# Forming the low part of every fourth weight chunk with an accumulating transfer

## The chip, the cores and the metric

The kernel runs on one core of a Trainium2 chip. The metric is the device time of one execution in microseconds. Three runs of the kernel before the change took 1153.44, 1153.44 and 1154.11 us.

## What is computed

The kernel computes two layers of a streaming encoder on 256 rows of 1024 values, all in float32. Each layer is a feed-forward block, a mixer (a state-space scan, chunk attention and gates, all fed by one input projection) and a second feed-forward block. Each of the three has a norm before it and a norm after it.

```python
for l in range(DEPTH):                       # DEPTH = 2
    f1 = swiglu(rmsnorm(x, g[0]), w_gate, w_up, w_down)
    x = x + 0.5 * rmsnorm(f1, g[1])
    m = hybrid_mixer(rmsnorm(x, g[2]), w_in, ..., w_o)
    x = x + rmsnorm(m, g[3])
    f2 = swiglu(rmsnorm(x, g[4]), w_gate, w_up, w_down)
    x = x + 0.5 * rmsnorm(f2, g[5])
```

## The kernel before

All large products run on TensorE in the format fp32r. To keep float32 accuracy, each float32 matrix is split in two: a high part, which is the matrix rounded to fp32r, and a low part, which is the matrix minus its high part. A product then takes three matmuls: high by high, high by low, low by high.

The weights come from memory in 368 chunks of 128 x 1024 float32 values (512 KB each). `weight(i)` (line 443) makes one chunk ready: SyncE loads it into a buffer `raw` (line 452), ScalarE rounds it into `wh` (line 454, through `act`, line 358), and VectorE writes `wl = raw - wh` (line 455, through `tt`, line 365). There are 4 buffers `raw`, 8 buffers `wh` and 8 buffers `wl`. The loads are issued in the order of the chunks, on SyncE's queue.

The 256 rows are two tiles of 128, t = 0 and t = 1. Each chunk is used once by each tile, with six matmuls of 512 columns each time; the first one that reads `wl` is the second of the six. Tile 1 works on a chunk three chunks after tile 0 (`LAG = 3`), so that one tile's matmuls run while the other tile's norm, transposes or activations are under way.

Nothing of the order is written by hand. The code first records all operations in a graph; `schedule` (line 197) then simulates five queues (TensorE, ScalarE, VectorE, GpSimd and the loads) with a cost for each operation, a latency for each pair of engines and a due time that is counted back from the matmuls. Of the operations that can start, the one with the earliest due time goes first. The order in which this plan starts the operations becomes each engine's program order. Chunk conversions are due a margin of 7.558 us (`MARGIN["conv"]`) before the matmul that needs them. GpSimd's part is small: it sets buffers, and in each norm it raises one value per row to the power -1/2 (`pow`, line 376), between VectorE's sum and VectorE's scaling.

Of the kernel before, what the change touches and what calls it, by code (L numbers as in the profile page):

```python
# [12 lines left out]
F32 = mybir.dt.float32  # L13
# [3 lines left out]
AF = mybir.ActivationFunctionType  # L17
ALU = mybir.AluOpType
# [31 lines left out]
HOP = 0.2  # L50
DMA_LAT = 2.1
DMA_RATE = 350e3


class Buf:
# [6 lines left out]
class View:  # L62
# [50 lines left out]
    def ap(self):  # L113
        t = self.buf.tile
        for s in self.steps:
            t = s(t)
        return t
# [11 lines left out]
class Graph:  # L129
# [62 lines left out]
    def latency(self, a, b):  # L192
        if a.eng == "dma":
            return DMA_LAT if b.eng != "dma" else 0.0
        return LAT.get((a.eng, b.eng), HOP)

    def schedule(self):
        for o in reversed(self.ops):
            d = 1e9
            for s in o.succ:  # L200
                m = MARGIN.get(o.stream, 0.0) if s.stream != o.stream else 0.0
                d = min(d, s.due - m - o.cost - self.latency(o, s))
            o.due = d if o.due is None else max(o.due - CAP, min(o.due, d))
            o.wait = len(o.deps)
            o.est = 0.0
        queue = {c: [] for c in ORDERED}
        for o in sorted(self.ops, key=lambda o: (o.due, o.n)):
            for b in o.bufs:
                if b.cls in queue and b.order is None:
                    queue[b.cls].append(b)  # L210
                    b.order = len(queue[b.cls])
        self.taken = {c: [False] * (len(q) + 1) for c, q in queue.items()}
        self.low = {c: 1 for c in queue}
        free = {e: 0.5 for e in ("pe", "act", "dve", "pool", "dma")}
        slots = {c: [0.0] * n for c, n in SLOTS.items()}
        cand = {e: [] for e in free}
        for o in self.ops:
            if not o.wait:
                cand[o.eng].append(o)
        table, order, left = None, [], len(self.ops)  # L220
        while left:
            best = None
            for e, lst in cand.items():
                t = None
                for o in lst:
                    s = max(free[e], self.fits(o, slots))
                    if t is None or s < t:
                        t = s
                if t is not None and t < 1e9 and (best is None or t < best[0]):
                    best = (t, e)  # L230
            if best is None:
                raise RuntimeError(f"no operation can start, {left} left")
            t, e = best
            pick = None
            for o in cand[e]:
                s = max(t, self.fits(o, slots))
                if s <= t + (LOOK if o.cost < 0.9 else 0.0):
                    key = (o.due + (s - t), o.n)
                    if pick is None or key < pick[0]:
                        pick = (key, o, s)  # L240
            _, o, s = pick
            cand[e].remove(o)
            cost = o.cost
            if o.func is not None and table not in o.func:
                cost += 1.28
                table = o.func[0]
            if e == "pe" and s < COLD:
                cost *= 2
            o.start, o.end = s, s + cost
            free[e] = o.end  # L250
            for b in o.bufs:
                if b.slot is not None:
                    continue
                if b.cls in slots:
                    fs = slots[b.cls]
                    i = min(range(len(fs)), key=lambda q: fs[q])
                    b.slot = i
                    fs[i] = 1e9
                    if b.cls in self.taken:
                        tk = self.taken[b.cls]  # L260
                        tk[b.order] = True
                        while self.low[b.cls] < len(tk) and tk[self.low[b.cls]]:
                            self.low[b.cls] += 1
                else:
                    b.slot = 0
                    if b.cls not in slots:
                        slots[b.cls] = [1e9]
            for b in o.bufs:
                b.left -= 1
                b.end = max(b.end, o.end + (DMA_LAT if e == "dma" else HOP))  # L270
                if not b.left:
                    slots[b.cls][b.slot] = b.end
            for q in o.succ:
                q.wait -= 1
                q.est = max(q.est, o.end + self.latency(o, q))
                if not q.wait:
                    cand[q.eng].append(q)
            order.append(o)
            left -= 1
        self.total = max(o.end for o in order)  # L280
        order.sort(key=lambda o: o.start)
        return order
# [29 lines left out]
class Kern:  # L312
# [24 lines left out]
    def dma(self, out, in_, after=()):  # L337
        n = math.prod(out.shape if not isinstance(out, View) else (out.parts[1] - out.parts[0], *out.idx.shape))
        isv = isinstance(out, View)
        return self.g.op("dma", 4 * n / DMA_RATE, [out] if isv else [], [] if isv else [in_],  # L340
                         lambda: self.nc.sync.dma_start(out=ap(out), in_=ap(in_)), after=after)  # L341

    def memset(self, eng, out, v, after=()):
        name = "gpsimd" if eng == "pool" else "vector"
        self.g.op(eng, 0.1 + out.free_size() / (1100 if eng == "pool" else 1080), [out], [],
                  lambda: getattr(self.nc, name).memset(out.ap(), v), after=after)
# [96 lines left out]
    def weight(self, i):  # L443
        if i not in self.ws:
            g = self.g
            keep = (g.stream, g.rank, g.due)
            self.mode("conv" if i >= 6 else "conv0", "main")
            raw = g.buf("raw", [P, 1024])
            wh, wl = g.buf("wh", [P, 1024], F32R), g.buf("wl", [P, 1024], F32R)
            parts = [slice(0, 512), slice(512, 1024)] if i < 2 else [slice(0, 1024)]  # L450
            for s in parts:
                self.last_raw = self.dma(raw[:, s], self.w_d[i][:, s], after=[self.last_raw] if self.last_raw else [])
            for s in parts:
                self.act(wh[:, s], raw[:, s], AF.Copy)
                self.tt(wl[:, s], raw[:, s], wh[:, s].bitcast(F32), ALU.subtract)
            self.ws[i] = (wh, wl)
            g.stream, g.rank, g.due = keep
        return self.ws[i]
# [685 lines left out]
```

## Time and profile before

| | us |
|---|---|
| median of 3 runs | 1153.44 |
| lowest and highest run | 1153.44, 1154.11 |
| span of the profiled execution, first to last instruction | 1151.6 |
| median of the runs less that span | 1.8 |

The span is that of one execution taken by the profiler; the runs' times hold, besides, what lies before the first and after the last instruction. In the profile, PE is TensorE's matmuls and PEld its weight loads, DVE is VectorE, ACT is ScalarE, POOL is GpSimd and SP is SyncE, which only issues transfers here. L365 is line 365 of the kernel. Lines such as L358 and L365 are helpers, so that a group of instructions is told by the names of what it writes and reads: `wl<-raw,wh` reads `raw` and `wh` and writes `wl`.

### The profile page before, as it was taken

The page shows a single profiled execution, that of the slowest core. Times are in us where ns is not written, and L with a number is a line of the kernel's source. Part 1 is how long each engine was busy: PE and PEld are TensorE (multiplying, and loading weights), DVE is VectorE, ACT ScalarE, POOL GpSimd, SP SyncE. Part 2 cuts the span into 40 slices and gives each one's busy share as a digit, 9 for nine tenths or more (in the row PEclk, how much of TensorE's full clock was granted, in tenths as well). Part 3 has the DMA queues.
Part 4 walks back from the last instruction along what each step waited for, and adds up shares of the span by engine and source line. Part 5 has one row for each costly group of instructions (what it writes and reads, how often), then busy time and mean ns, then how long its engine had stood idle before and what let it go on. Part 6 is the DMA issues. An engine that isn't in the chain of part 4 may idle for free.

```text
span 1151.6 us, 15538 instructions
## 1 busy us (share of the span) xinstructions
PE 1140.8 (99%) x5872; PEld 914.0 (79%) x5872; DVE 788.6 (68%) x1190; ACT 606.3 (53%) x894; POOL 19.8 (2%) x53
## 2 busy tenths in 40 slices
PE   8999999999999999999999999999999999999997
PEld 7887888877788888888888878887777888888886
DVE  6995557896958854655799734578779678544553
ACT  6565445648555554444555643455685446444442
POOL 1000000000000000000000000000000000000000
PEclk9999999999999999999999999999999999999999
DMA  8754565553255665555565546654534565555551
GB/s 291 252 195 159 183 219 166 181 164 130 86 189 178 207 200 184 186 182 184 187 220 193 184 150 200 204 177 147 166 110 145 184 198 163 192 192 181 190 165 37
DMA packets 60267, 205.02 MB, mean 178 GB/s; under 512 B 7072, under 2 KB 7840, under 8 KB 60192
## 3 DMA queue, kind: packets, MB, share of 16 engines
q1 hardware_dynamic: 60192, 204.03, 53.7%
q8 instruction: 46, 0.75, 0.3%
q14 instruction: 29, 0.24, 0.1%
HBM read 202.96 MB, written 1.05 MB: 177 GB/s over the span
## 4 chain that ended last, share of the span: by engine, by line
PE 94%; ACT 4%; issue 1%; DMA 0%; SPq 0%; DVE 0%; POOLq 0%; POOL 0%; DVEq 0%
PE ps L400 89%; PE ps L414 4%; ACT utz L358 2%; PE ps L406 1%; ACT blk L358 1%; ACT wh L358 1%; DMA x<-in_x_dram 0%; SPq L341 0%; DVE x L380 0%; POOLq L1139 0%; POOL s L376 0%; DVEq L1139 0%; DVE s L388 0%; POOLq L376 0%
## 5 line engine op out<-in xcount | busy, mean ns | idle before, releaser
L400 PE MATMUL ps<-wh,blk 128*128 128x512 f32 x2944 | 916.4, 400 | 0.0
L400 PEld LDWEIGHTS ps<-wh,blk 128*128 128x128 f32 x2944 | 548.0, 188 | 122.6 <-issue 0.3
L365 DVE TENSOR_TENSOR wl<-raw,wh 128x1024 fp32r<-128x1024 f32 (+1 forms) x370 | 448.7, 1217 | 281.9 <-ACT wh L358 280.6
L358 ACT ACTIVATE wh<-raw 128x1024 fp32r<-128x1024 f32 (+1 forms) x370 | 389.7, 1055 | 374.5 <-PE ps L400 334.1
L400 PE MATMUL ps<-wl,blk 128*128 128x512 f32 x1472 | 551.7, 399 | 0.0
L400 PEld LDWEIGHTS ps<-wl,blk 128*128 128x128 f32 x1472 | 274.8, 188 | 61.1 <-issue 0.3
L358 ACT ACTIVATE blk<-ps 128x512 fp32r<-128x512 f32 (+3 forms) x136 | 78.1, 583 | 121.5 <-PE ps L414 103.3
L365 DVE TENSOR_TENSOR blk<-ps,blk 128x512 fp32r<-128x512 f32 (+2 forms) x104 | 69.0, 666 | 36.1 <-ACT blk L358 34.9
L414 PE MATMUL ps<-ident,blk 128*128 128x128 f32 x432 | 76.8, 273 | 0.2
L414 PEld LDWEIGHTS ps<-ident,blk 128*128 128x128 f32 x432 | 57.0, 140 | 20.1 <-ACT blk L358 1.0
L358 ACT ACTIVATE blk<-ps,s 128x512 f32<-128x512 f32 (+1 forms) x80 | 52.5, 658 | 27.6 <-PE ps L400 25.6
L380 DVE SCALAR_TENSOR_TENSOR blk<-ps,s,blk 128x512 f32<-128x512 f32 (+1 forms) x48 | 33.8, 703 | 15.3 <-PE ps L400 11.5
L376 POOL TENSOR_TENSOR s<-s,mhalf 128x1 f32<-128x1 f32 x24 | 13.8, 574 | 804.0 <-DVE s L388 799.1
L358 ACT ACTIVATE blk<-blk,s 128x128 f32<-128x128 f32 (+1 forms) x64 | 25.8, 444 | 0.0
L400 PEld LDWEIGHTS ps<-utz,bt 128*128 128x128 f32 x128 | 18.1, 191 | 4.0 <-ACT utz L358 2.8
L365 DVE TENSOR_TENSOR blk<-blk,blk 128x512 f32<-128x512 f32 (+3 forms) x38 | 21.1, 577 | 0.1
L358 ACT ACTIVATE utz<-blk 32x128 f32<-32x128 f32 x64 | 20.1, 314 | 1.0
L358 ACT ACTIVATE blk<-blk 64x128 f32<-64x128 f32 (+2 forms) x44 | 17.1, 393 | 6.5 <-DVE blk L380 6.0
L365 DVE TENSOR_TENSOR blk<-blk,e 128x512 f32<-128x512 f32 x32 | 20.3, 677 | 0.0
L400 PE MATMUL ps<-utz,bt 128*128 128x128 f32 x128 | 19.2, 278 | 1.0 <-ACT utz L358 0.8
L365 DVE TENSOR_TENSOR blk<-ps,e 128x512 f32<-128x512 f32 x32 | 19.9, 677 | 0.0
L856 DVE TENSOR_TENSOR_SCAN blk<-mt,blk 128x512 f32<-128x512 f32 x16 | 18.6, 1203 | 0.0
(106 smaller groups left out, 349.2 us busy)
## 6 DMA issues: line engine op xcount, KB each, us to landing
raw<-in_wall_dram SPq DMA_DIRECT2D x366, 512.0 KB, 3.5
gain<-in_gains_dram SPq DMA_DIRECT2D x22, 256.0 KB, 4.6
blk<-in_bias_dram SPq DMA_DIRECT2D x8, 256.0 KB, 5.0
raw<-in_wall_dram SPq DMA_DIRECT2D x4, 256.0 KB, 3.5
blk<-in_sp_dram SPq DMA_DIRECT2D x4, 256.0 KB, 4.0
x<-in_x_dram SPq DMA_DIRECT2D x3, 256.0 KB, 5.5
out_dram<-x SPq DMA_DIRECT2D x2, 256.0 KB, 2.0
out_dram<-x SPq DMA_DIRECT2D x2, 192.0 KB, 2.1
```

Of the source, the lines that this page charges most:

```text
L358: self.nc.scalar.activation(out=out.ap(), in_=in_.ap(), func=func, **k)
L365: lambda: self.nc.vector.tensor_tensor(out=out.ap(), in0=a.ap(), in1=b.ap(), op=op))
L376: lambda: self.nc.gpsimd.tensor_tensor(out=out.ap(), in0=a.ap(), in1=b.ap(), op=ALU.pow))
L380: return self.g.op("dve", cost, [out], [a, s, b], lambda: self.nc.vector.scalar_tensor_tensor(out=out.ap(), in0=a.ap(), scalar=ap(s), in1= ...
L400: return self.g.op("pe", cost, [out], [lhsT, rhs], lambda: self.nc.tensor.matmul(out.ap(), lhsT=lhsT.ap(), rhs=rhs.ap(), start=start, stop ...
L406: self.nc.tensor.matmul(out.ap(), lhsT=lhsT.ap(), rhs=rhs.ap(), start=start, stop=stop)
L414: lambda o=o, s=s: self.nc.tensor.transpose(o.ap(), s.ap(), self.ident.ap()))
L856: self.g.op("dve", 0.6, [o], [mt, z], lambda o=o, z=z: self.nc.vector.tensor_tensor_scan(out=o.ap(), data0=mt.ap(), data1=z.ap(), initial= ...
```

## The change

From chunk 16 on, every fourth chunk (i = 16, 20, ..., 364: 88 of the 368) gets its low part in another way. ScalarE still rounds `raw` into `wh`. ScalarE then writes `-wh` into `wl`, and GpSimd issues a transfer from `raw` to `wl` that adds what it carries to what stands there, so that `wl` becomes `raw - wh`. VectorE's subtraction is left out for these chunks. The planner is told of the new operation: it costs GpSimd 1.2 us, and what waits for it (TensorE's matmuls on `wl`, the next load into `raw`) may go 6.0 us after that.

```diff
+ADD_LAT = 6.0
...
     def latency(self, a, b):
         if a.eng == "dma":
             return DMA_LAT if b.eng != "dma" else 0.0
+        if a.func == "dma":
+            return ADD_LAT
         return LAT.get((a.eng, b.eng), HOP)
...
-            if o.func is not None and table not in o.func:
+            if e == "act" and o.func is not None and table not in o.func:
...
-                b.end = max(b.end, o.end + (DMA_LAT if e == "dma" else HOP))
+                b.end = max(b.end, o.end + (DMA_LAT if e == "dma" else ADD_LAT if o.func == "dma" else HOP))
...
+    def dma_add(self, out, in_):
+        return self.g.op("pool", 1.2, [out], [out, in_],
+                         lambda: self.nc.gpsimd.dma_start(out=out.ap(), in_=in_.ap(), accum_op=ALU.add), func="dma")
...
+            if i >= 16 and i % 4 == 0:
+                self.act(wh, raw, AF.Copy)
+                self.act(wl, wh.bitcast(F32), AF.Copy, scale=-1.0)
+                self.dma_add(wl.bitcast(F32), raw)
+                parts = []
             for s in parts:
                 self.act(wh[:, s], raw[:, s], AF.Copy)
                 self.tt(wl[:, s], raw[:, s], wh[:, s].bitcast(F32), ALU.subtract)
```

## Rows read from the trace of the kernel before

**Rows 1.** The page: span, then each engine's busy time, share, instructions.

```profile
span 1151.6 us, 15538 instructions
PE 1140.8 (99%) x5872; PEld 914.0 (79%) x5872; DVE 788.6 (68%) x1190; ACT 606.3 (53%) x894; POOL 19.8 (2%) x53
```

**Rows 2.** The page: the chain that ended last, by engine.

```profile
PE 94%; ACT 4%; issue 1%; DMA 0%; SPq 0%; DVE 0%; POOLq 0%; POOL 0%; DVEq 0%
```

**Rows 3.** Waits of PEld and PE: total us, times, longest us.

```profile
PEld ps L400 <- issue: 10.2, 38, 0.4
PEld ps L414 <- DMA x<-in_x_dram: 3.1, 3, 2.0
PEld ps L400 <- ACT utz L358: 2.8, 6, 0.7
PEld ps L414 <- ACT blk L358: 1.0, 2, 0.5
PEld ps L406 <- DVE blk L365: 0.7, 2, 0.4
PEld ps L406 <- DVE wl L365: 0.4, 1, 0.4
PEld ps L400 <- DVE wl L365: 0.2, 1, 0.2
PE ps L400 <- ACT utz L358: 0.8, 2, 0.4
```

**Rows 4.** Groups by line and shape: count | busy us, mean ns | idle before.

```profile
L365 DVE TENSOR_TENSOR wl<-raw,wh 128x1024 fp32r<-128x1024 f32 x366 | 446.0, 1223 | 278.9 <-ACT wh L358 277.7 <-issue 0.3
L358 ACT ACTIVATE wh<-raw 128x1024 fp32r<-128x1024 f32 x366 | 387.2, 1059 | 371.6 <-PE ps L400 334.1 <-issue 15.8 <-DMA raw<-in_wall_dram 14.6
L376 POOL TENSOR_TENSOR s<-s,mhalf 128x1 f32<-128x1 f32 x24 | 13.8, 574 | 804.0 <-DVE s L388 799.1 <-DVE blk L365 4.9
```

**Rows 5.** Timeline of ACT: start us, us, what, idle before and its releaser.

```profile
320.60 1.06 ACT L358 ACTIVATE wh<-raw 128x1024 fp32r<-128x1024 f32 x1 [0.64 <-PE ps L400]
321.56 0.67 ACT L358 ACTIVATE blk<-ps,s 128x512 f32<-128x512 f32 x1
...
440.12 1.06 ACT L358 ACTIVATE wh<-raw 128x1024 fp32r<-128x1024 f32 x1 [1.72 <-PE ps L400]
442.90 1.06 ACT L358 ACTIVATE wh<-raw 128x1024 fp32r<-128x1024 f32 x1 [1.72 <-PE ps L400]
445.68 1.06 ACT L358 ACTIVATE wh<-raw 128x1024 fp32r<-128x1024 f32 x1 [1.72 <-PE ps L400]
```

**Rows 6.** Timelines of PE and DVE in the same stretch.

```profile
442.93 0.39 PE L400 MATMUL ps<-wl,blk 128*128 128x512 f32 x1
443.16 0.39 PE L400 MATMUL ps<-wh,blk 128*128 128x512 f32 x1
443.39 0.40 PE L400 MATMUL ps<-wl,blk 128*128 128x512 f32 x1
...
441.21 1.23 DVE L365 TENSOR_TENSOR wl<-raw,wh 128x1024 fp32r<-128x1024 f32 x1 [1.56 <-ACT wh L358]
```

**Rows 7.** Issues by kind: KB each, median us to landing; queue; landings of `raw`.

```profile
raw<-in_wall_dram SPq DMA_DIRECT2D x366, 512.0 KB, 3.5
gcol<-in_g_dram SPq DMA_DIRECT2D x1, 4.0 KB, 1.6
...
q1 hardware_dynamic: 60192, 204.03, 53.7%
...
L341 SPq DMA_DIRECT2D raw<-in_wall_dram x370: 327/328/921, 1.6 to 1117.7; - x185
...
DMA to landing us min/median/max: 2.6/3.5/8.0
```

**Rows 8.** Waits of SP's queue and of ACT's conversions.

```profile
SPq L341 <- DVE wl L365: 820.4, 313, 15.9
...
ACT wh L358 <- PE ps L400: 334.1, 237, 3.0
```

**Rows 9.** Windows: busy us (and count) of each engine, PEclk, DMA share, GB/s.

```profile
core 0: us, PE busy (x) PEld busy (x) DVE busy (x) ACT busy (x) POOL busy (x), PEclk, DMA share, GB/s
225.00:296.00 71.00, 70.92 (x494) 54.90 (x494) 57.37 (x98) 48.34 (x105) 0.55 (x1) 1.00 0.38 127
410.00:560.00 150.00, 150.00 (x669) 121.23 (x668) 85.40 (x115) 67.39 (x73) 0.00 (x0) 1.00 0.56 188
793.00:864.00 71.00, 70.92 (x493) 55.04 (x492) 57.27 (x97) 48.34 (x105) 0.55 (x1) 1.00 0.39 127
```

**Rows 10.** The same windows for `wl` alone: subtractions stand under DVE.

```profile
225.00:296.00 71.00, 28.76 (x70) 13.16 (x70) 19.39 (x17) 1.00 0.38 127
...
793.00:864.00 71.00, 28.34 (x69) 12.98 (x69) 19.27 (x16) 1.00 0.39 127
```

## The prediction

> **What bounds the kernel now.** I read the page's busy shares first: PE is busy 99% of a span of 1151.6 us, DVE 68%, ACT 53% and POOL 2% [rows 1]. A busy share alone proves little, so the chain that ended last comes next: 94% of it is PE, 4% ACT, and DVE rounds to 0% [rows 2]. Then the waits of the matmul engine, which say what PE could win at all [rows 3]: after the inputs' arrival (3.1 us) it waited for ACT 2.8 + 1.0 + 0.8 us and for DVE 0.7 + 0.4 + 0.2 us in the rows shown, some 6 us in all, and the longest single wait was 0.7 us. The 10.2 us under "issue" are PE's own. PE runs at its upper clock level, 2.4 GHz (granted share 1.00 in the windows, [rows 9]), and in a dense stretch one 512-column matmul follows the other every 0.23 us [rows 6]. So the reader is to see a kernel that ends when PE has gone through its list, with hardly a gap in it.
>
> The conversions run ahead of PE and are held back by it: 237 of ACT's roundings into `wh` waited for PE, 334.1 us in all [rows 8], that is for a `wh` buffer that PE had not yet let go. In a dense stretch one chunk is rounded every 2.78 us (440.12, 442.90, 445.68; [rows 5]), which is PE's pace of 12 matmuls per chunk at 0.23 us [rows 6].
>
> **What the change removes.** 88 subtractions of 1223 ns each [rows 4]: 107.6 us of DVE. DVE is hardly on the chain [rows 2], and PE's waits for it come to 1.3 us [rows 3]. I put the gain at 0; its upper bound is 1.3 us directly, and about 6 us if a less loaded DVE also shortened every wait for ACT.
>
> **What it adds on ACT.** 88 copies `-wh` of the shape of the rounding, 1059 ns each [rows 4], though the next instruction starts 0.96 us after one (320.60 to 321.56, [rows 5]): 84 to 93 us, which brings ACT from 53% to about 61%. In dense stretches this is covered by ACT's idle time: in 410 to 560 us it is busy 67.4 of 150 us [rows 9] and would be so about 80, with 13 more copies. Cover is thin in one stretch of each layer, 225 to 296 and 793 to 864 us, where ACT is busy 48.3 of 71 us and DVE 57.4 [rows 9]. There 17 and 16 subtractions stand [rows 10], so 4 copies land in each stretch, 8 in all, 8 x 1.06 = 8.5 us if each were in PE's way, 0 if none is. For the value between I let the 93 us fall on the chain as ACT's work there does now, 4% [rows 2]: 3.7 us; and I take half of it, 1.8 us, because the planner sees ACT's cost and sets other matmuls before a late one. This half is a choice, not a row.
>
> **What it adds on GpSimd's queue and the transfer engines.** No row shows a transfer issued by GpSimd or one that adds. Issue: SP's take 0.33 us, the longest 0.92 [rows 7], and GpSimd's own small instruction 0.57 [rows 4]; the planner's entry in the diff is 1.2 us, and I take that, the most careful of them. Landing: a 4 KB load lands 1.6 us after its issue and a 512 KB load 3.5 us (2.6 to 8.0) [rows 7], so 512 KB in one stream cost 1.9 us over a fixed 1.6. An addition reads two streams and writes one. One stream's price is 3.5 us, two are 1.6 + 2 x 1.9 = 5.4, three one after the other 7.3; the lower end is the fastest load, 2.6, the upper end the slowest load with two more streams, 8.0 + 3.8 = 11.8. I take 5.4, since a plain load too reads and writes within its one stream.
>
> The Trainium skill, page "Collectives: The Full Stack", section "The bandwidth ceiling: the fold count and why AG ≠ RS ≠ AR", says that an add in the transfer engines costs two source reads and no time for the addition itself. No run here shows that yet. The page "DMA: Bandwidth & Descriptors", section "Anatomy of one DMA — SWDGE (gpsimd) path", gives a GpSimd transfer 2.0 us and its bytes at 436 GB/s; an estimate from this page with 1 MB read is 4.4 us, and the chain below would be 7.7 us by it.
>
> **Is the low part there in time?** The chain of such a chunk: ACT rounds (0.96 until the next may start), ACT copies (1.06), a hand-over (DVE starts 0.03 us after ACT's end, 441.18 to 441.21, [rows 5, 6]; I take 0.1), GpSimd issues (1.2), the transfer lands (5.4). Sum: 8.7 us after the start of the rounding, where the subtraction was done after 2.3 us (440.12 to 442.44, [rows 5, 6]). The time that it has: 8 buffers `wh`, of which a chunk holds one from tile 0's use until tile 1 is done with it, 3 chunks of lag and the chunk itself, 4 periods. That leaves 4 periods of 2.78 us = 11.1 us from rounding to first use, plus 0.23 us because only the second matmul reads `wl`: 11.3 us. Spare 2.6 us. So the change hides if the landing comes within 11.3 - 3.3 = 8.0 us of the end of the issue. The planner besides makes these chunks due 7.2 us earlier than the others (1.2 + 6.0 in the diff), so that they may overtake a chunk or two where their `raw` is there.
>
> **Buffers.** `raw` is let go by the landing in place of the subtraction, and SP stands at that door already: 313 of its issues waited for a subtraction, 820.4 us [rows 8]. Four chunks have 4 buffers x 4 periods = 44.5 us of `raw`; three of them need 3.5 + 2.3 = 5.8 us each, the fourth 3.5 + 8.7 = 12.2, together 29.6 us. For `wh` and `wl` it is 8 x 4 x 2.78 = 89 us against 3 x (2.3 + 11.1) + (8.7 + 11.1) = 60. Both fit. Behind SP's waiting issue stand the next loads, and behind those the next roundings; with 14.9 us spare in four periods they are not late. The transfer engines are 53.7% busy with 204 MB [rows 7]; 88 x 512 KB read twice are 92 MB, at the same rate 24% more, 78%: it fits.
>
> **What is queued behind GpSimd's new waits.** GpSimd waits for ACT's copy, then issues; behind it may stand a norm's power, 24 in all [rows 4], on which the next stage's transposes depend. With 88 x 1.2 = 106 us, GpSimd is busy 9% of the span, so about 2 of the 24 meet an issue and lose half of one, 0.6 us each; PE fills most of that with the other tile. I cost it at 0.
>
> **Sum.** Before, in the runs, 1153.44 us, which is 1.8 us over the profiled span of 1151.6; I carry these 1.8 us over unchanged. 1151.6 + 1.8 - 0 (DVE) + 1.8 (ACT) + 0 (late landings) + 0 (GpSimd's queue) = 1155.2 us. A difference under 0.2%, 2.3 us, is about what a measurement of this kernel cannot tell from none.
>
> **The rivals.**
>
> *Late landings* (slower). If the landing takes longer than 8.0 us after the issue, each of the 88 chunks is late by the rest and PE, in order, stands: at 9 us all of them would cost 88 x 1.0 = 88 us, 1243. Since the planner lets such a chunk overtake, I expect the stall in about a quarter of them, 22 us: 1177 us. At the bound of 11.8 us it is 88 x 3.8 = 334 us, 1488, if nothing is overtaken. For it speaks that additions share the engines with loads, of which the slowest took 8.0 us; against it the spare of 2.6 us at 5.4. A second way to the same place: GpSimd's issue may have to find gaps in DVE's work, and with DVE busy 68% [rows 1] the 1.2 us stretch to 1.2 / 0.32 = 3.75, and the chain to 11.2 us, all the spare. The page "SBUF — State Buffer" of the Trainium skill, section "SBUF: two separate sides", warns of such a trap: a transfer from GpSimd stands while VectorE holds the port that both share. Chance 0.23.
>
> *ACT in the way* (slower). The copies fall in front of evacuations that PE waits for, in the two thin stretches and at the norms: at the 8.5 us bound the time is 1162. It decides from 2.3 us on, three copies in PE's way. For it speaks that ACT is the only other engine on the chain [rows 2]; against it that the planner counts these copies. Chance 0.19.
>
> *GpSimd in the way* (slower). If an issue takes 4 us, GpSimd is busy 31%, 7 of 24 powers lose 2 us each: 14 us, 1168 at most. It decides from about 1.5 us an issue, if nothing fills the wait. Chance 0.06.
>
> *DVE's relief counts* (faster). The two thin stretches are those where DVE too is busiest, 57.4 of 71 us, and 8 subtractions, 9.8 us, leave them. If all of PE's 6 us of waits went, the time is 1147; it decides from 2.3 us on. Against it: no wait was above 0.7 us. Chance 0.07.
>
> **How the numbers follow.** My forecast, hidden but for ACT, has 0.45: 1155.2 us, its own range 1152.5 to 1157. Of this 0.45 some 0.04 lie above 0.2% and 0.01 below; so faster is 0.07 + 0.01 = 0.08, slower 0.23 + 0.19 + 0.06 + 0.04 = 0.52, and the same 0.40. The range of 8 in 10 leaves out the relief (0.07) below and half of the late landings (0.12) above: 1152 to 1178 us.
>
> **What would show it.** DVE should be busy near 680 us, ACT near 700, with 88 fewer `wl<-raw,wh`. The page's list of issues should give the adding transfer's landing, below 8 us after the issue for my forecast; the waits of PE should show few rows for that transfer. PE waiting for it dozens of times means late landings; PE waiting longer for ACT's `utz` or `blk` means ACT in the way; DVE or ACT waiting for POOL's power means GpSimd in the way. The prediction is wrong above all if the landing is much slower than two streams' price.

## The result, and the profile after

The changed kernel takes 1168.49 us (median of 4 runs, 1166.68 to 1169.43) against 1153.44 us before: the ratio is 1.0127, with a 95% interval of 1.0113 to 1.0142. That is 15 us slower. It lies in the stated range (1152 to 1178), but not where the forecast put its likeliest case (1155.2): the transfer was to be hidden, and something was not. Of the experiments below, three had one execution each that took 1873 to 2883 us, where the others of the same kernel agree within 0.1%: the medians count it, the ratios leave it out, and in the run with the measured latency, where it is the profiled one, only the order of the instructions is read.

The page of the changed kernel: span, busy shares, the chain by engine and by line, queues, two groups, and issues with their landing. Line numbers have moved by 3 to 7: L358, L365, L376, L380 and L400 of before are L365, L372, L383, L387 and L407 here.

```profile
span 1167.7 us, 15788 instructions
PE 1147.4 (98%) x5872; PEld 915.3 (78%) x5872; DVE 685.0 (59%) x1102; ACT 694.2 (59%) x982; POOL 97.5 (8%) x141
...
q1 hardware_dynamic: 60192, 204.03, 51.9%
q0 software_dynamic: 12672, 46.14, 21.5%
...
PE 89%; ACT 4%; DMA 2%; issue 2%; DVE 1%; SPq 0%; POOL 0%; POOLq 0%; DVEq 0%; ACTq 0%
...
L348 POOL DMA_DIRECT2D wl<-raw x88 | 76.4, 868 | 950.4 <-ACT wl L365 855.6
L365 ACT ACTIVATE wl<-wh 128x1024 fp32r<-128x1024 f32 x88 | 93.2, 1060 | 2.4
...
raw<-in_wall_dram SPq DMA_DIRECT2D x366, 512.0 KB, 4.0
wl<-raw POOLq DMA_DIRECT2D x88, 512.0 KB, 4.8
```

The costs of the parts are near what was worked out. DVE lost 103.6 us and ACT gained 87.9 [rows 1]. GpSimd issues in 0.87 us and the addition has landed 4.8 us after the start of the issue, where I had 1.2 + 5.4 = 6.6. But PE's share of the chain fell from 94% [rows 2] to 89%, and "DMA" has come into it with 2%. So the reader should look for PE standing, and for whom. The waits of the changed kernel (total us, times, longest), and below them one of the kernel before:

```profile
ACT wh L365 <- DMA raw<-in_wall_dram: 46.3, 28, 4.4
...
PE ps L421 <- DVE blk L387: 3.2, 2, 1.8
...
PE ps L407 <- ACT blk L365: 2.6, 5, 0.9
...
PE ps L421 <- ACT blk L365: 1.8, 2, 0.9
```

```profile
ACT wh L358 <- DMA raw<-in_wall_dram: 17.5, 19, 1.8
```

Two things are to be seen. No row in which PE waits names the adding transfer: the low part was there each time. And PE now waits for evacuations (`blk` from ACT) and for the norm (`blk` from DVE, L387), while ACT's waits for loads into `raw` have gone from 17.5 us to 46.3. The windows of [rows 9], and one behind the last of them, help to say where:

```profile
225.00:296.00 71.00, 68.91 (x480) 52.58 (x479) 52.43 (x92) 51.67 (x109) 4.08 (x5) 1.00 0.58 168
...
410.00:560.00 150.00, 150.00 (x667) 121.29 (x666) 69.70 (x101) 83.75 (x90) 11.79 (x14) 1.00 0.81 234
...
868.00:876.00 8.00, 6.15 (x48) 4.57 (x46) 8.00 (x17) 7.56 (x17) 0.00 (x0) 1.00 0.00 0
```

In the dense stretch PE is busy all the time, with 667 instructions against 669 before: 14 transfers there cost nothing that shows. In the first mixer it is busy 68.91 us of 71, against 70.92. In the second the changed kernel is already more than 8 us behind, so the window 793 to 864 us ends before the place that loses: that lies in 868 to 876 us, where PE is busy 6.15 us of 8.

**The first place, the mixer.** ACT's timeline, then PE's, then two windows of 4 us, in the first layer's mixer:

```profile
282.09 1.05 ACT L365 ACTIVATE wl<-wh 128x1024 fp32r<-128x1024 f32 x1
283.04 2.59 ACT L365 ACTIVATE utz<-blk 32x128 f32<-32x128 f32 x8
...
287.64 2.61 ACT L365 ACTIVATE utz<-blk 32x128 f32<-32x128 f32 x8
...
293.21 2.49 ACT L365 ACTIVATE blk<-blk,s 128x256 f32<-128x256 f32 x6
295.60 0.67 ACT L365 ACTIVATE blk<-ps,s 128x512 f32<-128x512 f32 x1
...
293.75 1.64 PE L421 MATMUL ps<-ident,blk 128*128 128x128 f32 x8 [0.87 <-ACT blk L365]
296.32 0.50 PE L407 MATMUL ps<-wh,blk 128*128 128x512 f32 x1 [0.93 <-ACT blk L365]
...
292.00:296.00 4.00, 2.52 (x16) 1.48 (x15) 4.00 (x10) 4.00 (x10) 0.00 (x0) 1.00 0.00 0
296.00:300.00 4.00, 3.68 (x12) 2.68 (x12) 4.00 (x7) 2.34 (x6) 0.00 (x0) 0.61 0.00 0
```

ACT is busy 4.00 of 4.00 us and gets to the evacuation `blk<-ps,s` only at 295.60, behind both runs of `utz` (the state-space work) and most of the softmax work; the next matmul on weights starts 0.7 us later. Between the two stalls PE's eight transposes take 1.64 us: before each of the last three pairs the weight load waits 0.20 us for ACT again, so PE is counted as busy while it goes at ACT's pace. TensorE had been busy 2.52 of 4 us when it was granted 0.61 in the next four, so part of that time ran at the lower level of 1.2 GHz. Before the change the same evacuation came directly behind the last of the `utz` work and ahead of the second half of the softmax work; the timeline of ACT of the kernel before:

```profile
286.47 0.96 ACT L358 ACTIVATE utz<-blk 32x128 f32<-32x128 f32 x3
287.45 0.69 ACT L358 ACTIVATE blk<-ps,s 128x512 f32<-128x512 f32 x1
```

**The second place, a norm.** SP's issues, ACT and PE at the first norm behind the mixer:

```profile
376.67 0.81 SPq L344 DMA_DIRECT2D gain<-in_gains_dram  x2
377.80 4.94 SPq L344 DMA_DIRECT2D raw<-in_wall_dram  x4
...
385.24 1.06 ACT L365 ACTIVATE wh<-raw 128x1024 fp32r<-128x1024 f32 x1 [4.11 <-DMA raw<-in_wall_dram]
386.33 1.06 ACT L365 ACTIVATE wl<-wh 128x1024 fp32r<-128x1024 f32 x1
387.30 0.58 ACT L365 ACTIVATE blk<-ps 128x512 bf16<-128x512 f32 x1
...
390.72 0.66 PE L421 MATMUL ps<-ident,blk 128*128 128x128 f32 x4 [1.42 <-DVE blk L387]
```

The load of chunk 120 is the first of the four: it goes out behind the two loads of `gain` and lands at 385.16, 7.4 us after its issue. ACT stands 4.11 us on it, then rounds, then copies, and only then comes to the norm's squares (387.30). PE has run out of matmuls by then and idles 1.42 us. In the second layer the same place costs 1.77 us. Before the change the load of chunk 120 went out ahead of those two and landed 3.5 us later, and its rounding waited for no load:

```profile
369.14 0.33 SPq L341 DMA_DIRECT2D raw<-in_wall_dram  x1
370.34 0.80 SPq L341 DMA_DIRECT2D gain<-in_gains_dram  x2
...
376.22 1.06 ACT L358 ACTIVATE wh<-raw 128x1024 fp32r<-128x1024 f32 x1 [1.68 <-PE ps L400]
```

**The third, the end.** The last instruction of the chain in each kernel, the changed one first, with GpSimd's closing DRAIN (shortest, median and longest ns; first and last start):

```profile
1163.09 0.26 DVE x L387
...
L1151 POOLq DRAIN  x3: 34/102/5693, 1161.2 to 1167.4; - x3
```

```profile
1148.25 0.26 DVE x L380
...
L1139 POOLq DRAIN  x3: 34/78/651, 1146.4 to 1151.3; - x3
```

From its end to the end of the span it is 1167.7 - 1163.35 = 4.3 us after, and 1151.6 - 1148.51 = 3.1 before: 1.2 us more, in a stretch in which no engine computes. GpSimd's longest DRAIN takes 5.69 us in place of 0.65 and ends at 1166.9, behind SyncE's last issue and its DRAIN (1165.9). The traces of the runs below agree: that DRAIN and the stretch behind the last instruction are 0.65 and 3.1 us with the copies alone, 1.0 and 3.3 with four transfers, 5.1 and 3.7 with 54.

### The profile page after: what moved, and what is told of

Read it like the earlier page. It is cut to its first block, busy times and chain, and to the rows that moved or that the text cites. A ratio compares the mean times of both kernels' runs of the same rounds, so it can differ in the third digit from the quotient of the medians.

```text
span 1167.7 us, 15788 instructions
## 1 busy us (share of the span) xinstructions
PE 1147.4 (98%) x5872; PEld 915.3 (78%) x5872; DVE 685.0 (59%) x1102; ACT 694.2 (59%) x982; POOL 97.5 (8%) x141
## 3 DMA queue, kind: packets, MB, share of 16 engines
q1 hardware_dynamic: 60192, 204.03, 51.9%
q0 software_dynamic: 12672, 46.14, 21.5%
## 4 chain that ended last, share of the span: by engine, by line
PE 89%; ACT 4%; DMA 2%; issue 2%; DVE 1%; SPq 0%; POOL 0%; POOLq 0%; DVEq 0%; ACTq 0%
PE ps L407 84%; PE ps L421 4%; DMA raw<-in_wall_dram 2%; ACT blk L365 2%; ACT utz L365 2%; PE ps L413 2%; ACT wh L365 1%; DMA x<-in_x_dram 1%; DVE wl L372 0%; DVE blk L372 0%; DVE blk L387 0%; SPq L344 0%; ACT wl L365 0%; POOL s L383 0%; DVE x L387 0%
## 5 line engine op out<-in xcount | busy, mean ns | idle before, releaser
L407 PE MATMUL ps<-wh,blk 128*128 128x512 f32 x2944 | 917.2, 400 | 2.6 <-ACT blk L365 2.6
L407 PEld LDWEIGHTS ps<-wh,blk 128*128 128x128 f32 x2944 | 547.6, 188 | 127.4 <-ACT blk L365 5.0
L365 ACT ACTIVATE wh<-raw 128x1024 fp32r<-128x1024 f32 (+1 forms) x370 | 389.7, 1055 | 336.4 <-PE ps L407 286.0
L407 PE MATMUL ps<-wl,blk 128*128 128x512 f32 x1472 | 551.1, 398 | 0.0
L372 DVE TENSOR_TENSOR wl<-raw,wh 128x1024 fp32r<-128x1024 f32 (+1 forms) x282 | 342.1, 1216 | 283.9 <-ACT wh L365 283.1
L407 PEld LDWEIGHTS ps<-wl,blk 128*128 128x128 f32 x1472 | 274.9, 188 | 62.1 <-issue 0.7
L348 POOL DMA_DIRECT2D wl<-raw x88 | 76.4, 868 | 950.4 <-ACT wl L365 855.6
L365 ACT ACTIVATE blk<-ps 128x512 fp32r<-128x512 f32 (+3 forms) x136 | 77.4, 580 | 95.2 <-PE ps L421 79.9
L372 DVE TENSOR_TENSOR blk<-ps,blk 128x512 fp32r<-128x512 f32 (+2 forms) x104 | 69.3, 667 | 91.1 <-ACT blk L365 90.7
L365 ACT ACTIVATE wl<-wh 128x1024 fp32r<-128x1024 f32 x88 | 93.2, 1060 | 2.4
L365 ACT ACTIVATE blk<-ps,s 128x512 f32<-128x512 f32 (+1 forms) x80 | 51.8, 658 | 17.1 <-PE ps L407 14.0
L387 DVE SCALAR_TENSOR_TENSOR blk<-ps,s,blk 128x512 f32<-128x512 f32 (+1 forms) x48 | 33.7, 703 | 43.1 <-PE ps L407 39.4
L365 ACT ACTIVATE blk<-blk,s 128x128 f32<-128x128 f32 (+1 forms) x64 | 25.8, 442 | 0.1
L383 POOL TENSOR_TENSOR s<-s,mhalf 128x1 f32<-128x1 f32 x24 | 16.2, 675 | 94.5 <-DVE s L395 73.7
L372 DVE TENSOR_TENSOR blk<-ps,e 128x512 f32<-128x512 f32 x32 | 19.9, 678 | 5.4 <-PE ps L407 5.4
L387 DVE SCALAR_TENSOR_TENSOR blk<-blk,ps 128x512 f32<-128x512 f32 x20 | 13.6, 682 | 13.0 <-ACT blk L365 9.8
L372 DVE TENSOR_TENSOR blk<-blk,blk 128x512 f32<-128x512 f32 (+3 forms) x38 | 20.8, 577 | 0.1
L365 ACT ACTIVATE utz<-blk 32x128 f32<-32x128 f32 x64 | 20.1, 315 | 0.9
L372 DVE TENSOR_TENSOR blk<-blk,e 128x512 f32<-128x512 f32 x32 | 20.3, 680 | 0.0
L407 PEld LDWEIGHTS ps<-utz,bt 128*128 128x128 f32 x128 | 17.0, 191 | 3.6 <-ACT utz L365 2.8
```

The source lines that it names most:

```text
L348: lambda: self.nc.gpsimd.dma_start(out=out.ap(), in_=in_.ap(), accum_op=ALU.add), func="dma")
L365: self.nc.scalar.activation(out=out.ap(), in_=in_.ap(), func=func, **k)
L372: lambda: self.nc.vector.tensor_tensor(out=out.ap(), in0=a.ap(), in1=b.ap(), op=op))
L383: lambda: self.nc.gpsimd.tensor_tensor(out=out.ap(), in0=a.ap(), in1=b.ap(), op=ALU.pow))
L387: return self.g.op("dve", cost, [out], [a, s, b], lambda: self.nc.vector.scalar_tensor_tensor(out=out.ap(), in0=a.ap(), scalar=ap(s), in1= ...
L407: return self.g.op("pe", cost, [out], [lhsT, rhs], lambda: self.nc.tensor.matmul(out.ap(), lhsT=lhsT.ap(), rhs=rhs.ap(), start=start, stop ...
```

## The experiments

Three theories were set against each other. **R**: the adding transfer holds `raw` until it lands, loads start late, and ACT stands on them. **O**: the copies on ACT, or the new order, cost time. **Q**, formed after eight runs: a few of the 88 chunks fall where the planner then gives an evacuation a bad seat; the others cost little. Each ratio is to the kernel before on the same chip, with its 95% interval.

**No transfer, the same order.**

```diff
-        lambda: self.nc.gpsimd.dma_start(out=out.ap(), in_=in_.ap(), accum_op=ALU.add), func="dma")
+        lambda: None, func="dma")
```

> The changed kernel with its plan and every engine's order kept, but GpSimd issues no transfer, so that the low parts of the 88 chunks hold -wh alone (the addition is left out) and raw is free after ScalarE's rounding. Theory R (raw is held until the landing, loads start late and bunched, ScalarE stands on a load in front of a norm): the stalls at the norms after the mixers (near 389 and 964 us, 4.5 us together) go, and the loads land in 3.5 us again; about 1163 us if the rest is the order's. Theory O (the new order and the copies on ScalarE make the loss in the two mixer stretches): those 9 us stay, at the same place, between 280 and 320 and between 860 and 880 us. If the transfer made everything: 1154 us, if the order and the copies made everything: 1168.

1166.7 us (1164.14 to 1168.11), ratio 1.0111 [1.0096, 1.0126]. Nearly the whole loss is there without a transfer. PE's timeline shows both stalls of the mixer, a little smaller one at the norm:

```profile
292.81 1.64 PE L421 MATMUL ps<-ident,blk 128*128 128x128 f32 x8 [0.87 <-ACT blk L365]
295.38 0.50 PE L407 MATMUL ps<-wh,blk 128*128 128x512 f32 x1 [0.93 <-ACT blk L365]
...
387.48 0.66 PE L421 MATMUL ps<-ident,blk 128*128 128x128 f32 x4 [0.90 <-DVE blk L387]
```

So what the transfer does on the chip costs some 2 us of the 15 (1168.49 - 1166.70 = 1.8, with intervals that overlap); the order that was planned for it, with the copies, costs the rest. The stall at the norm is in that order too: here too the load of chunk 120 stands behind the two loads of `gain` and takes 6.8 us to land.

**Six raw buffers.** `"raw": 4` becomes `"raw": 6` in the changed kernel.

> The changed kernel with 6 raw buffers in place of 4; the planner knows of them. Theory R: loads are no longer late, ScalarE's waits for loads fall from 46 us to about 17 as before the change, the stalls at the norms go: 1163 us or below, since the plan too is free to order the mixers anew. Theory O (copies on ScalarE are in the way, buffers don't matter): 1166 to 1170 us.

1156.46 us, ratio 1.0025 [1.0014, 1.0035]: 12 of the 15 us are gone, as R allowed and O did not. The waits and ACT's timeline show both places healed, the evacuation back near 288:

```profile
ACT wh L365 <- DMA raw<-in_wall_dram: 6.4, 4, 3.1
...
288.60 0.69 ACT L365 ACTIVATE blk<-ps,s 128x512 f32<-128x512 f32 x1
```

**The old order with the new work.** The plan of the kernel before; one planned operation issues both new ones.

```diff
+    def neg_add(self, out, a, b):
+        def fn():
+            self.nc.scalar.activation(out=out.ap(), in_=b.bitcast(F32).ap(), func=AF.Copy, scale=-1.0)
+            self.nc.gpsimd.dma_start(out=out.bitcast(F32).ap(), in_=a.ap(), accum_op=ALU.add)
+        return self.g.op("dve", 0.07 + a.free_size() / 960, [out], [a, b], fn)
...
+            if i >= 16 and i % 4 == 0:
+                self.act(wh, raw, AF.Copy)
+                self.neg_add(wl, raw, wh)
+                parts = []
```

> The kernel before with its plan untouched, so TensorE's order is the old one; where the plan starts the subtraction of every fourth chunk, the copy -wh goes into ScalarE's order and the adding transfer into GpSimd's. Theory O in the form that the new order is to blame: near 1155 us, the mixer stretches as before. Theory O in the form that the copies are to blame wherever they stand, or that the plan must know of the landing: 1165 us or more, with stalls of TensorE on the transfer or on ScalarE. Theory R: the norms lose some 4 us here too, since raw is held as long.

1192.25 us, ratio 1.0330 [1.0315, 1.0345]. Here R is seen in full: SP's queue waits for nearly every transfer, ACT stands on loads, and PE does wait for low parts. The waits:

```profile
SPq L341 <- DMA wl<-raw: 713.4, 87, 11.9
...
ACT wh L358 <- DMA raw<-in_wall_dram: 145.3, 55, 7.4
...
PE ps L407 <- DMA wl<-raw: 6.5, 5, 2.0
```

The largest of PE's waits are for the norm there (DVE `blk`, L387: 11.7 us). So the old order is no cure. The new order avoids most of what the landing would cost, and pays for it in the mixers.

**The dense stretches alone.**

```diff
-            if i >= 16 and i % 4 == 0:
+            if i >= 16 and i % 4 == 0 and not 60 <= i % 184 < 128:
```

> The changed kernel with the accumulating transfer for 54 chunks only, those converted in the dense feed-forward stretches; the chunks around both mixers and the norms beside them keep the subtraction. Both theories: within 2 us of the kernel before, 1153 to 1156 us, with about 1 us at the end. If the mere number of transfers counts, 54/88 of 15 us: 1162.

1154.37 us, ratio 1.0007 [0.9997, 1.0016]. 54 transfers where PE is fed by a steady run of chunks cost nothing that can be measured.

**The measured latency in the planner.** The issue's cost 1.2 becomes 0.87, `ADD_LAT` 6.0 becomes 3.9.

> The changed kernel with the planner told what the trace measured: 0.87 us for GpSimd's issue and 3.9 us from its end to the landing, 4.8 in place of 7.2 us. Theory R (raw is held too long, in the plan and on the chip): the plan holds raw for 2.4 us less of its 7 us extra, so it gives back a third to a half of the 15 us: 1160 to 1164 us. Theory O (the copies on ScalarE cost): unchanged, 1166 to 1170 us.

1162.55 us, ratio 1.0075 [1.0058, 1.0092]: 6 us come back, as R gave. The work on the chip is the same; only the plan is another. But the order of ACT in its trace has the evacuation of the mixer where the changed kernel has it, behind both runs of `utz` and the softmax work:

```profile
548.87 2.59 ACT L365 ACTIVATE utz<-blk 32x128 f32<-32x128 f32 x8
...
560.18 0.67 ACT L365 ACTIVATE blk<-ps,s 128x512 f32<-128x512 f32 x1
```

So the 6 us came back elsewhere, and the time that is left is near that of the four transfers below (1161.82).

**The copies alone.**

```diff
-                self.dma_add(wl.bitcast(F32), raw)
+                self.tt(wl, raw, wl.bitcast(F32), ALU.add)
```

> The copies on ScalarE alone: for the same 88 chunks ScalarE writes -wh into wl, and VectorE adds raw to it in place of the subtraction; no transfer, so raw is held about 1 us longer than before the change. Theory R: 1153 to 1156 us. Theory O (88 copies of 1.06 us in ScalarE's order are what costs): 1162 us or more.

1154.57 us, ratio 1.0008 [0.9998, 1.0017]. 88 copies on ACT cost nothing by themselves. The one in the mixer is there, and the evacuation comes 3 us later than before the change, not 8 (ACT's timeline):

```profile
280.29 1.05 ACT L365 ACTIVATE wl<-wh 128x1024 fp32r<-128x1024 f32 x1
...
290.42 0.67 ACT L365 ACTIVATE blk<-ps,s 128x512 f32<-128x512 f32 x1
```

**The kernel before with 6 and with 3 raw buffers.** `"raw": 4` becomes 6, then 3, with nothing else changed.

> The kernel before the change with 6 raw buffers, nothing else: the control for the changed kernel with 6. Theory R: raw is not short here, so the same time, 1152.5 to 1154.5 us, and the changed kernel's 3 us over the kernel before are the copies, the transfers and the end. If two more buffers are a gain by themselves, it shows here: below 1151 us.

1153.67 us, ratio 0.9997 [0.9988, 1.0007]: more buffers are no gain by themselves.

> The kernel before the change with 3 raw buffers, no transfer and no copy: takes away 11.1 us of raw in four chunks, where the change takes away some 5 to 7. Theory R: slower than the changed kernel or about as slow, 1165 to 1185 us, with ScalarE waiting for loads, and the loss in the mixers and at the norms, not in the dense stretches. Theory O: 1153 to 1156 us.

1155.39 us, ratio 1.0016 [1.0007, 1.0026]. R expected 1165 or more and fell here. ACT waits for loads as long as in the changed kernel, and it hardly matters:

```profile
ACT wh L358 <- DMA raw<-in_wall_dram: 49.0, 46, 3.8
```

**Other chunks, as many.** `i % 4 == 0` becomes `i % 4 == 3`.

> The changed kernel with the same number of transfers, 88, but for the chunks i = 19, 23, ..., 367 in place of 16, 20, ..., 364. Theory Q (a few of the chunks fall where the plan then seats an evacuation of ScalarE behind a run of state-space and softmax work, and others in front of a norm; the rest cost nothing): the loss depends on which chunks are chosen, here below 4 us: 1153 to 1158. Theory R as first put (every transfer holds raw too long): the same loss as the change, 1165 to 1170 us.

1158.99 us, ratio 1.0045 [1.0030, 1.0060]: 5 us in place of 15 for the same 88 transfers, a little above what Q gave, far below R. In this plan the evacuation of the first mixer starts at 288.69, in its old place.

**Four transfers.**

```diff
-            if i >= 16 and i % 4 == 0:
+            if i % 184 in (88, 92):
```

> The change for two chunks of each layer alone, 88 and 92 of the layer's 184, which are converted in the mixer where ScalarE is busiest: 4 transfers in place of 88. Theory Q: these four make the loss in the mixers, 1161 to 1165 us, with the evacuation near 288 us seated some 8 us later, behind the run of state-space and softmax work. Theory R as first put: 4/88 of the loss, 1154 to 1155 us.

1161.82 us, ratio 1.0066 [1.0051, 1.0081]. Four transfers make 7.9 of the 15 us. ACT's and PE's timelines show the bad seat and both stalls again:

```profile
294.20 0.67 ACT L365 ACTIVATE blk<-ps,s 128x512 f32<-128x512 f32 x1
...
292.35 1.64 PE L421 MATMUL ps<-ident,blk 128*128 128x128 f32 x8 [0.89 <-ACT blk L365]
294.92 0.72 PE L407 MATMUL ps<-wh,blk 128*128 128x512 f32 x1 [0.93 <-ACT blk L365]
```

**All but those four.** `i % 184 not in (88, 92)` is added to the condition of the changed kernel.

> The change for all its chunks but those four: 84 transfers. Theory Q: the mixers are as before the change, what is left is the norms' 4 us and the end's 1 us: 1157 to 1160 us. Theory R as first put: 84/88 of the loss, 1167 to 1169 us.

1160.23 us, ratio 1.0052 [1.0035, 1.0068], at the upper end of what Q gave. The evacuation is back at 288.42; the stall at the norm is still there (ACT's and PE's timelines):

```profile
288.42 0.69 ACT L365 ACTIVATE blk<-ps,s 128x512 f32<-128x512 f32 x1
...
385.27 0.66 PE L421 MATMUL ps<-ident,blk 128*128 128x128 f32 x4 [1.37 <-DVE blk L387]
```

The two parts add up: 1161.82 - 1153.91 = 7.9 and 1160.23 - 1153.91 = 6.3, together 14.2 of the 15 us. The traces say where. Counting PE's matmuls on weights in order, this table gives how much later they start than in the kernel before, as medians in the stretches 100 to 190, 335 to 365, 440 to 700, 885 to 905 and 990 to 1100 us of that kernel and at the end of the span, and how much each stage adds (us, of the profiled executions):

| | start | first mixer | norm behind it | second mixer | norm behind it | end | sum |
|---|---|---|---|---|---|---|---|
| changed kernel | 0.8 | 5.4 | 2.3 | 4.1 | 2.2 | 1.3 | 16.1 |
| no transfer, same order | -0.1 | 3.8 | 1.5 | 3.9 | 1.3 | 0.4 | 10.8 |
| four transfers | 0.3 | 4.5 | -0.2 | 4.6 | -0.1 | 0.3 | 9.4 |
| all but those four | 0.1 | 0.8 | 2.7 | 0.6 | 1.6 | 1.3 | 7.1 |

The four transfers lose in the mixers and almost nothing elsewhere; the other 84 lose mostly at the two norms and at the end. The 0.8 us of the changed kernel's start are there at 10 us already, before GpSimd's first transfer (42.5 us), and are no effect of the change.

**Nine `wh` and nine `wl`, `raw` left at 4.**

> The changed kernel with 9 buffers wh and 9 wl in place of 8, raw left at 4. Theory R (raw alone is short): no better than 1165 us. Theory Q (the plan needs room anywhere in the conversions to keep ScalarE's evacuations in their old seats): 1154 to 1158 us, as with 6 raw buffers.

1155.17 us, ratio 1.0011 [1.0002, 1.0020]. Room in another class of buffers heals as well as room in `raw`. ACT waits for loads even longer than in the changed kernel:

```profile
ACT wh L365 <- DMA raw<-in_wall_dram: 50.9, 28, 7.1
```

With it R, which names `raw` alone, is out, and Q stands. That slack is what heals is not shown apart from the mere fact that each of these runs has a new plan: the other 88 chunks, without any slack, keep the evacuation in its old place too. No version ran measurably faster than the kernel before; the changed ones that come nearest are the dense-only one (1.0007), the copies alone (1.0008) and the nine buffers (1.0011).

## Why the prediction was right or wrong

**The range** held by luck. Its upper part was put there for late landings, which did not come. The forecast itself was 1155.2 us, ACT's rival was bounded at 1162, and the rival that was bounded at 1168, GpSimd, did not come either.

**What bounds the kernel** was right. PE's list sets the end; no run was faster, and DVE's relief of 103.6 us was worth nothing. The 6 us of PE's waits are some 5: PE's 0.8 us for `utz` are the same stalls as part of PEld's 2.8.

**The price of the transfer** was mis-sized to the safe side: 4.8 us from the start of the issue against 6.6. For the chunk of the norm above, the rounding starts at 385.24 and the issue at 387.69; with 4.8 us the low part is there 7.2 us after the start, against 8.7 worked out and 11.3 allowed. DVE's work did not stretch the issue either: the longest of the 88 took 1.04 us. *Late landings* did not happen. They do where the plan knows nothing of the landing, in the run with the old order. Per byte the additions took (21.5 / 46.14) / (51.9 / 204.03) = 1.83 times the engine time of the loads. The Trainium skill, page "Collectives: The Full Stack", section "The bandwidth ceiling: the fold count and why AG ≠ RS ≠ AR", says that an add needs two source reads and that these set its rate; 1.83, near two, agrees with it.

**GpSimd's queue** was right: 0.87 us an issue, and no wait for its power above 0.5 us in all in the changed kernel's list of waits.

**ACT** is where the forecast failed. The step was that 4% of the new 93 us, halved, lie in PE's way, "because the planner sees ACT's cost and sets other matmuls before a late one". It did not: with the transfers of chunks 88 and 92 in its plan it seated an evacuation 8 us later, behind `utz` and the softmax, and PE stood. The two mixers lost 5.4 and 4.1 us where 1.8 was allowed for the whole kernel. In the first layer the two stalls of 0.87 and 0.93 us are followed by four microseconds at 0.61 of the clock, by an estimate 4 x 0.39 = 1.6 us more. The rival *ACT in the way* (0.19) named the place (the thin stretches), the sign that came (PE waits longer for ACT's `blk`) and a bound of 1162 us; it was wrong on the means. The copies by themselves cost nothing that can be measured (1.0008), and the price came from the order, not from the copies' length.

**The buffers** were right on the average and wrong as an argument. Loads were not to be late "with 14.9 us spare in four periods". They are late at the norms all the same, because there chunk 120's load stands behind two others, and ACT takes its work in order. The prediction's sum has no term for this; the two places measured 2.3 and 2.2 us, of which 1.5 and 1.3 are there without a transfer on the chip. An average spare says nothing of the one place where a norm stands behind a load. Even so, lateness alone is cheap: the kernel before with 3 buffers waits as long for loads and loses 0.16%.

**The end** was not foreseen: the 1.8 us around the span were carried over, and 1.2 us were added inside it, behind the last work, with GpSimd's longer DRAIN.

What is shown: the plan made for the transfers, not the transfers on the chip, makes most of the loss; four transfers in the mixers make half of it; the rest comes from the other 84, mostly at the two norms and at the end; two more buffers `raw`, or one more `wh` and `wl`, remove nearly all. That the late evacuation is the cause in the mixers is read from the timelines: the changed plans whose first mixer has it by 290.5 us lose at most 1.6 us there, and those that have it from 294 us on lose 3.8 to 5.4. No run moves it alone. What stays open: by which of its comparisons the planner moves that evacuation. Telling it of a chain that is 2.4 us shorter gave back 6 us but did not move the evacuation, and no run separates the earlier due time from the longer hold of the buffers.

## What to carry to other kernels

Where one engine's list is full and a planner orders the rest, a new operation is to be priced by the seats that it takes in the in-order queues at the tightest place, not by its busy time or by an average of free buffers: 84 transfers cost no more here than four. Before such a change is judged, it is worth trying it with other chunks, and with one more buffer; if the time then falls back, the operation was not too slow; the plan made for it was at fault. Work that nobody waits for (DVE's subtractions) isn't worth moving.

## What the runs showed of the hardware that had not been expected

An adding transfer of 512 KB within the on-chip buffers, issued by GpSimd, took 0.87 us to issue and landed 4.8 us (median) after the issue began. The loads beside it landed in 4.0 us, 3.5 before [rows 7]; but they took 4.0 us too in the run with the copies alone, which has no such transfer. GpSimd's closing DRAIN grew with the number of its transfers, from 0.65 us with none to 5.69 with 88, and the end of the program became 1.2 us longer. In the first mixer a stretch with TensorE busy 2.52 of 4 us was followed by four microseconds with a granted share of 0.61, while in the second layer stalls of the same length (0.92 and 0.93 us) cost no clock: 868 to 876 us reads 1.00 with TensorE busy 6.15 of 8 us, and so does the stretch behind it. The same two stalls cost no clock in either layer in the run without transfers.
